# FFN tiles whose last step stands behind the next tile's partial sums, a convolution whose steps are spread later, and a pinned start with sixteen idle matmuls

## The chip, the core and the metric

The kernel runs on one core of a Trainium2 chip. The metric is the device time of one launch in microseconds. A core has five instruction streams that run side by side, each in its own order: TensorE (PE, matmuls), VectorE (DVE), ScalarE (ACT), GpSimd (POOL) and SyncE (SP, here a queue of DMA transfers; ACT issues some too). An instruction waits until what it reads has been written and what it overwrites has been read, and everything behind it in the same stream waits with it.

## What is computed

Two transformer-like blocks over 1024 positions and 1024 channels, in float32. Only the first is touched by more than a name; its part that matters, from the reference:

```python
h = rmsnorm(x, g_mix[i])
z = jnp.einsum("bsd,dn->bsn", h, w_in[i])
...
a = a_val * jax.nn.sigmoid(a_gt)
a = causal_dwconv(a, conv_a_w[i]) + conv_a_b[i]      # 31 taps, 512 channels
a = jax.nn.silu(layernorm(a, ln_a_g[i], ln_a_b[i]))
y_a = jnp.einsum("bsc,cd->bsd", a, w_a_out[i])
s = sc_b * causal_dwconv(sc_c * sc_v, conv_b_w[i])   # 3 taps
y_b = jnp.einsum("bsc,cd->bsd", s, w_b_out[i])
x = x + jnp.einsum("bsd,de->bse", g_a * y_a + g_b * y_b, w_o[i])
h = rmsnorm(x, g_ffn[i])
u = jnp.einsum("bsd,df->bsf", h, w_up[i])
f_gate = causal_dwconv(u[..., :D_FF], conv_f_w[i]) + conv_f_b[i]    # 3 taps, D_FF = 2816
f = jax.nn.gelu(f_gate, approximate=True) * u[..., D_FF:]
x = x + jnp.einsum("bsf,fd->bsd", f, w_down[i])
```

## The kernel before

Channels lie on the 128 partitions, positions along the free axis, in two halves of 512. Every product is made exact enough by splitting both operands into a high and a low part (wh, wl for weights; hh, hl and the like for data): three fp32r matmuls of 128x512 for each pair of blocks (lines 134 to 136, `mm3`). A weight comes by DMA into a buffer `wr` (5 of them), ACT copies it to wh, and DVE or POOL subtracts to give wl.

*The start.* SP loads the small vectors (`vec`, 325 columns, line 103), then for each of 8 channel blocks a weight (line 261) and half of x (line 262); the second half of x follows (line 268). ACT writes w0h (L264) and hh (L154), DVE writes w0l (L265) and hl (L155), and PE runs the first products `agt`.

*The convolutions.* The 31 taps of the long convolution are 30 steps of DVE on a whole row of 1024 for each of 4 tiles (`acc`, line 321) after one first step on ACT (L330). They are put into a queue; `bg(n)` takes n of them, so the numbers in the calls say where they stand between the other work. That other work is: `scc`, `scv`, `scb` products for 4 tiles, evicted by DVE into `cc` (L533, L539) and `sv` (L548), with a short convolution (first step on ACT, L328; two steps on DVE, L321; a multiplication on POOL, L543) between; then `split` of the four `sv` into sph (ACT, L151) and spl (DVE, L152), which are the operands of the products `yb`, eight times with a `gate` product ahead of each. The LayerNorm of the long convolution stands behind in the same queue of steps and is needed by the products `ya` after the gates.

*The FFN.* 22 tiles of 128 channels of both halves of `w_up`. A tile's four blocks are multiplied with a scheme of seven products instead of eight (a0, b0, b1, t4, t1, t2, t3; `quad`), each of 12 matmuls. The sums of weights that the scheme needs are four POOL additions (L635 to L638, for the tile after), and the weights are split in four groups, named here by their buffers qa (a0, t2), qb (t3, t1), qc (b0, b1) and qe (t4): ACT L151 and DVE L152. Products share PSUM banks, with additions on DVE between (L686: the u2, u4, c21, c22 and the second half of ug). PE's order in a tile is t2, t3, t1, b0, b1, t4, then a0 of the next. What becomes of a tile is `ff_tile`: ug is scaled (DVE L724 and L686, POOL L727), convolved with 3 taps (ACT L330, two DVE steps L321), put through Gelu (ACT L741), scaled (POOL L742), multiplied with c21 and c22 (DVE L744, two halves) and stored by a DMA of ACT's queue (`f_spill`, L745). The framework's scheduler turns the written order into the order on each engine, mostly by when an instruction was written.

Of the kernel before, what the change touches and what calls it, by code (L numbers as in the profile page):

```python
# [11 lines left out]
F32 = mybir.dt.float32  # L12
# [8 lines left out]
P = 128  # L21
# [3 lines left out]
KD = D // P  # L25
# [30 lines left out]
def block_kernel(ctx: ExitStack, tc: tile.TileContext, a: dict, out: bass.AP, dbg=None):  # L56
# [45 lines left out]
    vec = const.tile([P, NV], F32, name="vec")  # L102
    nc.sync.dma_start(out=vec, in_=a["vecs"])

# [7 lines left out]
    G.memset(ones, 1.0)  # L112
    junk = const.tile([P, CTX], F32, name="junk")


# [141 lines left out]

    w0 = [[slot("w0" + q, F32R, (P, 2, H2)) for _ in range(KD // 2)] for q in "hl"]
    for k in range(KD):
        raw = wtile("wr", (P, H2), F32, NWR)  # L260
        nc.sync.dma_start(out=raw, in_=a["w_in0"][k])
        nc.sync.dma_start(out=xs[0][k], in_=a["xT"][k * P : (k + 1) * P, hs(0)])
        hi, lo = (w[k // 2][:, k % 2, :] for w in w0)
        S.activation(out=hi, in_=raw, func=AF.Copy)  # L264
        V.tensor_tensor(out=lo, in0=raw, in1=f32(hi), op=ALU.subtract)  # L265
        split(h1[k][0][:, hs(0)], h1[k][1][:, hs(0)], xs[0][k], v("g_mix", k))
    for k in range(KD):
        nc.sync.dma_start(out=xs[1][k], in_=a["xT"][k * P : (k + 1) * P, hs(1)])
    first = [[bank("agt") for _ in range(4)], [None] * 4]

# [257 lines left out]
    for i in range(4):  # L528
        w = load_w(a["w_in"][12 + i], KD, lo_eng=G)
        cc = slot("cc")  # L530
        for h in range(2):
            ps = gemm(w, h1, h, "scc")
            V.tensor_tensor(out=cc[:, hs(h)], in0=ps, in1=rb[:, hs(h)], op=ALU.mult)  # L533
            G.tensor_tensor(out=cc[:, hs(h)], in0=cc[:, hs(h)], in1=rb[:, hs(h)], op=ALU.mult)
        bg(6)
        w = load_w(a["w_in"][16 + i], KD, lo_eng=G)
        for h in range(2):
            ps = gemm(w, h1, h, "scv")
            V.tensor_tensor(out=cc[:, hs(h)], in0=ps, in1=cc[:, hs(h)], op=ALU.mult)  # L539
        sv[i] = slot("sv")  # L540
        for f in conv_steps(cc, sv[i], "conv_b_w", 3, i):
            f()
        G.tensor_tensor(out=sv[i], in0=sv[i], in1=rb, op=ALU.mult)  # L543
        bg(4)
        w = load_w(a["w_in"][8 + i], KD, lo_eng=G)
        for h in range(2):
            ps = gemm(w, h1, h, "scb")
            V.tensor_tensor(out=sv[i][:, hs(h)], in0=ps, in1=sv[i][:, hs(h)], op=ALU.mult)  # L548
        bg(6)

    def gate(j):
        w = load_w(a["w_in"][20 + j], KD, lo_eng=G)
        g = slot("gate")
        for h in range(2):
            ps = gemm(w, h1, h, "gate")
            V.tensor_tensor(out=g[:, hs(h)], in0=ps, in1=rb[:, hs(h)], op=ALU.mult)
            S.activation(out=g[:, hs(h)], in_=g[:, hs(h)], func=AF.Sigmoid, bias=v("b_gate", j))
        return g

# [5 lines left out]
    for j in range(KD):  # L565
        g = gate(8 + j)
        bg(5)
        w = load_w(a["w_b_out"][j], 4, lo_eng=G, small_w=True)
# [6 lines left out]
    for j in range(KD):  # L575
        gA.append(gate(j))
        bg(6)
    while bgq:
# [132 lines left out]

    def quad(w, ug, x):

        y, z, u = (bank("q") for _ in range(3))
        m1, u2, u4, c21, c22 = (half_t("qm") for _ in range(5))
# [5 lines left out]
        padd(u4, y, m1)  # L721
        padd(c22, z, u4)
        product(x, w, "b0", True)
        V.tensor_tensor(out=ug[:, hs(0)], in0=x, in1=rb2[:, hs(0)], op=ALU.mult)  # L724
        product(u, w, "b1")
        padd(ug[:, hs(1)], u, u4)
        G.tensor_tensor(out=ug[:, hs(1)], in0=ug[:, hs(1)], in1=rb2[:, hs(1)], op=ALU.mult)  # L727
        product(z, w, "t4", True)
        padd(c21, z, u2)
        return c21, c22  # L730

    def begin(j):
        w, x = load_quad(a["w_upq"][j]), bank("q")
        product(x, w, "a0")
        return w, x

    def ff_tile(j, ug, cs):
        fa = slot("fa")
        for f in conv_steps(ug, fa, "conv_f_w", 3, j, v("conv_f_b", j)):
            f()  # L740
        S.activation(out=fa, in_=fa, func=AF.Gelu_apprx_tanh)  # L741
        G.tensor_tensor(out=fa, in0=fa, in1=rb2, op=ALU.mult)  # L742
        for h in range(2):
            V.tensor_tensor(out=fa[:, hs(h)], in0=cs[h], in1=fa[:, hs(h)], op=ALU.mult)  # L744
# [3 lines left out]
    cs = quad_first(wq0, ug)  # L748
    w, x = begin(1)
    st.spread(rb2, (1,))  # L750
    V.tensor_tensor(out=ug, in0=ug, in1=rb2, op=ALU.mult)
    ff_tile(0, ug, cs)
    for j in range(1, N_FF):
        ug = slot("ug")
        cs = quad(w, ug, x)
        if j + 1 < N_FF:
            w, x = begin(j + 1)
        ff_tile(j, ug, cs)
    def load_f(k):
# [232 lines left out]
    po_spill = dram.tile([512, T], F32, name="po_spill")  # L992
    cinv = const.tile([P, 4, 16], F32, name="cinv")
    nc.sync.dma_start(out=cinv, in_=a["cinv"])
    for i in range(4):
# [73 lines left out]
    def rope_table(row):  # L1069

        tab = slot("rtab", F32, (P, 2, 512))
        nc.sync.dma_start(out=tab, in_=a["rope"][row])
        g = const.tile([P, 64], F32, name=f"rg{row}")
        nc.sync.dma_start(out=g, in_=a["rope_g"][row])
        rg = const.tile([P, 64], F32, name=f"rgr{row}")
# [435 lines left out]
```

## Time and profile before

| | |
|---|---|
| median of 3 runs | 2020.9 us (2017.68 to 2021.72) |
| the profiled execution, its own time | 2018.58 us |
| its span (first to last instruction) | 2016.8 us |
| PE busy | 1936.9 us, 96% of the span, 8926 matmuls |
| DVE busy | 1374.4 us, 68% |
| ACT busy | 701.5 us, 35% |
| POOL busy | 608.4 us, 30% |
| DMA | 186.11 MB, mean 92 GB/s |
| granted TensorE clock, mean | 0.993 of full |

PE is busy nearly throughout, so what counts is where it isn't. Busy time is a rough word for PE: matmuls are pipelined, and a matmul that is reported with 0.39 us starts 0.23 us after the one before it. Lost time shows as idle time ahead of a matmul, as a larger distance between starts, or as a lower granted clock.

### The profile page before, as it was taken

The page shows a single profiled execution, that of the slowest core. Times are in us where ns is not written, and L with a number is a line of the kernel's source. Part 1 is how long each engine was busy: PE and PEld are TensorE (multiplying, and loading weights), DVE is VectorE, ACT ScalarE, POOL GpSimd, SP SyncE. Part 2 cuts the span into 40 slices and gives each one's busy share as a digit, 9 for nine tenths or more (in the row PEclk, how much of TensorE's full clock was granted, in tenths as well). Part 3 has the DMA queues.
Part 4 walks back from the last instruction along what each step waited for, and adds up shares of the span by engine and source line. Part 5 has one row for each costly group of instructions (what it writes and reads, how often), then busy time and mean ns, then how long its engine had stood idle before and what let it go on. Part 6 is the DMA issues. An engine that isn't in the chain of part 4 may idle for free.

```text
span 2016.8 us, 23964 instructions
## 1 busy us (share of the span) xinstructions
PE 1936.9 (96%) x8926; PEld 1575.9 (78%) x8926; DVE 1374.4 (68%) x2219; ACT 701.5 (35%) x1172; POOL 608.4 (30%) x417
## 2 busy tenths in 40 slices
PE   8999979999999999999998999999999999999999
PEld 6788758788877777777776787878777888888887
DVE  5799897345668765665655449996889476878751
ACT  5211121233344332332324312355442256556510
POOL 1334521131002545455451010223354322323200
PEclk9999989999999999999999999999999999999999
DMA  6011212212442222222225436544331221001151
GB/s 214 24 50 37 63 58 74 73 42 94 148 149 89 79 78 68 87 65 79 78 71 180 172 118 200 180 142 143 109 126 62 71 76 45 14 14 43 34 191 47
DMA packets 76468, 186.11 MB, mean 92 GB/s; under 512 B 8640, under 2 KB 15424, under 8 KB 76352
## 3 DMA queue, kind: packets, MB, share of 16 engines
q1 hardware_dynamic: 67856, 162.04, 24.9%
q10 hardware_dynamic: 8496, 22.55, 2.8%
q8 instruction: 70, 1.15, 0.2%
q14 instruction: 46, 0.38, 0.1%
HBM read 149.42 MB, written 35.13 MB: 92 GB/s over the span
## 4 chain that ended last, share of the span: by engine, by line
PE 48%; DVE 24%; issue 14%; POOL 6%; ACT 5%; DMA 3%; ACTq 0%; SPq 0%; POOLq 0%; DVEq 0%
DVE acc L321 6%; PE gate L135 3%; PE gate L134 3%; PE gate L136 3%; PE wd L135 2%; PE wd L136 2%; POOL ug L727 2%; PE wd L134 2%; POOL wr L635 2%; PE pv L1322 2%; DVE mj L432 2%; PE wout L134 1%; DVE wr L929 1%; PE wout L136 1%; PE wo L134 1%
## 5 line engine op out<-in xcount | busy, mean ns | idle before, releaser
L129 ACT ACTIVATE wh<-wr 128x1024 fp32r<-128x1024 f32 (+2 forms) x116 | 115.6, 997 | 342.5 <-PE wd L135 84.1
L130 POOL TENSOR_TENSOR wl<-wr,wh 128x1024 fp32r<-128x1024 f32 x44 | 115.8, 2634 | 269.3 <-ACT wh L129 249.1
L321 DVE SCALAR_TENSOR_TENSOR acc<-av,vec,acc 128x1023 f32<-128x1023 f32 (+14 forms) x120 | 192.0, 1600 | 4.3 <-ACT acc L330 1.7
L134 PE MATMUL q<-t,wh 128*128 128x512 f32 x352 | 140.5, 399 | 22.8 <-DVE qm L686 22.4
L151 ACT ACTIVATE wh<-wr 128x1024 fp32r<-128x1024 f32 (+1 forms) x92 | 84.5, 938 | 167.3 <-PE q L136 145.8
L135 PE MATMUL wd<-fl,wh 128*128 128x512 f32 x352 | 138.4, 395 | 2.6 <-DVE fl L763 2.5
L152 DVE TENSOR_TENSOR wl<-wr,wh 128x1024 fp32r<-128x1024 f32 (+1 forms) x92 | 113.9, 1239 | 37.7 <-ACT wh L151 37.6
L135 PE MATMUL q<-t,wh 128*128 128x512 f32 x352 | 138.9, 395 | 0.2 <-DVE t L152 0.2
L136 PE MATMUL q<-t,wl 128*128 128x512 f32 x352 | 138.7, 394 | 0.0
L136 PE MATMUL wd<-fh,wl 128*128 128x512 f32 x352 | 138.5, 395 | 0.0
L134 PE MATMUL wd<-fh,wh 128*128 128x512 f32 x352 | 132.5, 397 | 3.3 <-ACT fh L762 3.2
L221 POOL TENSOR_TENSOR ss<-ss,sq 128x512 f32<-128x512 f32 x42 | 62.3, 1499 | 201.5 <-ACT sq L220 201.5
L635 POOL TENSOR_TENSOR wr<-wr 128x512 f32<-128x512 f32 x22 | 45.2, 2053 | 208.6 <-DVE wl L152 101.8
L134 PEld LDWEIGHTS q<-t,wh 128*128 128x128 f32 x352 | 66.1, 188 | 46.6 <-issue 29.3
L134 PE MATMUL gate<-hh,wh 128*128 128x512 f32 x256 | 101.5, 396 | 0.0
L135 PE MATMUL gate<-hl,wh 128*128 128x512 f32 x256 | 101.1, 395 | 0.0
L136 PE MATMUL gate<-hh,wl 128*128 128x512 f32 x256 | 100.7, 393 | 0.0
L130 DVE TENSOR_TENSOR wl<-wr,wh 128x1024 fp32r<-128x1024 f32 (+2 forms) x72 | 83.8, 1164 | 16.2 <-ACT wh L129 15.1
L321 DVE SCALAR_TENSOR_TENSOR fa<-ug,vec,fa 128x1023 f32<-128x1023 f32 (+1 forms) x44 | 58.2, 1324 | 49.5 <-ACT fa L330 49.5
L744 DVE TENSOR_TENSOR fa<-qm,fa 128x512 f32<-128x512 f32 x44 | 28.4, 687 | 93.2 <-POOL fa L742 93.2
L1297 POOL TENSOR_SCALAR wr<-wr,rsum 128x1280 f32<-128x1280 f32 x32 | 43.0, 1345 | 145.6 <-DVE rsum L1296 128.2
L135 PEld LDWEIGHTS wd<-fl,wh 128*128 128x128 f32 x352 | 66.1, 188 | 20.2 <-DVE fl L763 4.4
(464 smaller groups left out, 5517.9 us busy)
## 6 DMA issues: line engine op xcount, KB each, us to landing
wr<-in_w_upq SPq DMA_DIRECT2D x88, 256.0 KB, 3.3
wr<-in_w_in SPq DMA_DIRECT2D x32, 512.0 KB, 3.4
wm<-in_w_modT SPq DMA_DIRECT2D x48, 256.0 KB, 3.0
f_spill<-fa ACTq DMA_DIRECT2D x22, 512.0 KB, 2.6
fl<-f_spill SPq DMA_DIRECT2D x22, 512.0 KB, 5.5
x<-in_xT SPq DMA_DIRECT2D x32, 256.0 KB, 4.5
wr<-in_w_o SPq DMA_DIRECT2D x16, 512.0 KB, 3.5
x_spill<-x ACTq DMA_DIRECT2D x32, 256.0 KB, 2.0
```

The lines of the kernel that those rows point to most:

```text
L129: S.activation(out=hi, in_=raw, func=AF.Copy)
L130: lo_eng.tensor_tensor(out=lo, in0=raw, in1=f32(hi), op=ALU.subtract)
L134: PE.matmul(ps, lh, rh, start=start, stop=False, **kw)
L135: PE.matmul(ps, lh, rl, start=False, stop=False, **kw)
L136: PE.matmul(ps, ll, rh, start=False, stop=stop, **kw)
L151: S.activation(out=hi, in_=src, func=AF.Copy)
L152: V.tensor_tensor(out=lo, in0=src, in1=f32(hi), op=ALU.subtract)
L221: eng.tensor_tensor(out=self.sums[:, hs(h)], in0=self.sums[:, hs(h)], in1=q, op=ALU.add)
L321: V.scalar_tensor_tensor(out=acc[:, s:T], in0=src[:, 0 : T - s], scalar=w, in1=acc[:, s:T], op0=ALU.mult, op1=ALU.add)
L432: V.scalar_tensor_tensor(out=half_t("mj"), in0=mm[n], scalar=1.0, in1=cb[ci][h], op0=ALU.mult, op1=ALU.mult, accum_out=modh[:, h, ci, j : ...
L635: G.tensor_tensor(out=s1, in0=a21, in1=a22, op=ALU.add)
L1297: G.tensor_scalar(out=pm, in0=pm, scalar1=rs, scalar2=1.0, op0=ALU.mult, op1=ALU.mult)
```

## The change

*The start.* Only the 8 columns of `vec` that the start needs (g_mix) are loaded first; the other 317 come after the second pair of loads. The loads are written under a manual order for SP, so that weights and x alternate to the end, and the small tables `cinv` and `rope_g`, which were loaded far later, are loaded there. Sixteen matmuls of 128x128 on a tile of ones, into a bank that nobody reads, stand first on PE.

*The convolutions.* `bg(6), bg(4), bg(6)` around the short convolutions become 5, 3, 5; `bg(5)` after a gate of `yb` becomes 4; in the later gates `bg(6)` behind each becomes three steps inside each half.

*The FFN.* `ff_tile` is cut into `ff_conv` (convolution, Gelu, POOL's scaling) and `ff_end` (multiplication with c21, c22 and the store). `ff_end` of a tile is written inside the next tile's `quad`, behind its u4 and c22. `begin(j + 1)`, the load, the sums and the product a0 of the next tile, is written ahead of t4.

```diff
@@
-    nc.sync.dma_start(out=vec, in_=a["vecs"])
+    nc.sync.dma_start(out=vec[:, 0:KD], in_=a["vecs"][:, 0:KD])
...
+    idle = bank("idle")
+    for _ in range(16):
+        PE.matmul(idle[:, 0:P], ones, ones, start=True, stop=True)
...
+    order = tc.manual_schedule(engines={mybir.EngineType.SP})
+    order.__enter__()
     for k in range(KD):
...
+        if k == 1:
+            nc.sync.dma_start(out=vec[:, KD:NV], in_=a["vecs"][:, KD:NV])
...
+    cinv = const.tile([P, 4, 16], F32, name="cinv")
+    nc.sync.dma_start(out=cinv, in_=a["cinv"])
+    rope_g = [const.tile([P, 64], F32, name=f"rg{row}") for row in range(2)]
+    for row in range(2):
+        nc.sync.dma_start(out=rope_g[row], in_=a["rope_g"][row])
+    order.__exit__(None, None, None)
...
-        bg(6)
+        bg(5)
...
-        bg(4)
+        bg(3)
...
-        bg(6)
-
-    def gate(j):
+        bg(5)
+
+    def gate(j, steps=0):
...
+            bg(steps)
...
-        bg(5)
+        bg(4)
...
-        gA.append(gate(j))
-        bg(6)
+        gA.append(gate(j, 3))
...
-    def quad(w, ug, x):
+    def quad(j, w, x, prev):
...
         padd(u4, y, m1)
         padd(c22, z, u4)
+        ff_end(*prev)
         product(x, w, "b0", True)
...
+        nxt = begin(j + 1) if j + 1 < N_FF else None
         product(z, w, "t4", True)
         padd(c21, z, u2)
-        return c21, c22
...
-    def ff_tile(j, ug, cs):
+        return ug, (c21, c22), nxt
+
+    def ff_conv(j, ug):
         fa = slot("fa")
...
         G.tensor_tensor(out=fa, in0=fa, in1=rb2, op=ALU.mult)
+        return fa
+
+    def ff_end(j, fa, cs):
         for h in range(2):
             V.tensor_tensor(out=fa[:, hs(h)], in0=cs[h], in1=fa[:, hs(h)], op=ALU.mult)
         nc.scalar.dma_start(out=f_spill[j * P : (j + 1) * P, :], in_=fa)
...
     for j in range(1, N_FF):
-        ug = slot("ug")
-        cs = quad(w, ug, x)
-        if j + 1 < N_FF:
-            w, x = begin(j + 1)
-        ff_tile(j, ug, cs)
+        ug, cs, nxt = quad(j, *nxt, prev)
+        prev = j, ff_conv(j, ug), cs
+    ff_end(*prev)
```

What the engines are given moves as follows. (In the rows, a name's number tells one buffer from another; the width after it is the shape.)

DVE in the convolution stage, just ahead of the last short convolution (`sv`), before; a step `acc` of width 1024 - s is step s of the third tile:

```order
L539 TENSOR_TENSOR cc_1391<-scv_1458,cc_1391 128x512
L321 SCALAR_TENSOR_TENSOR acc_714<-av_661,vec,acc_714 128x1006
L321 SCALAR_TENSOR_TENSOR acc_714<-av_661,vec,acc_714 128x1005
L321 SCALAR_TENSOR_TENSOR acc_714<-av_661,vec,acc_714 128x1004
L539 TENSOR_TENSOR cc_1391<-scv_1484,cc_1391 128x512
L321 SCALAR_TENSOR_TENSOR acc_714<-av_661,vec,acc_714 128x1003
L321 SCALAR_TENSOR_TENSOR sv_1510<-cc_1391,vec,sv_1510 128x1023
```

The same place of DVE in the changed kernel:

```order
L553 TENSOR_TENSOR cc_1409<-scv_1475,cc_1409 128x512
L335 SCALAR_TENSOR_TENSOR acc_741<-av_688,vec,acc_741 128x1015
L335 SCALAR_TENSOR_TENSOR acc_741<-av_688,vec,acc_741 128x1014
L335 SCALAR_TENSOR_TENSOR acc_741<-av_688,vec,acc_741 128x1013
L553 TENSOR_TENSOR cc_1409<-scv_1501,cc_1409 128x512
L335 SCALAR_TENSOR_TENSOR acc_741<-av_688,vec,acc_741 128x1012
L335 SCALAR_TENSOR_TENSOR sv_1527<-cc_1409,vec,sv_1527 128x1023
```

The last `sv` follows step 12 of the third tile instead of step 21. In ACT's order, the first step of that tile (which the others wait for) now stands behind the last `wsh`, a small weight of `yb` that waits for its DMA; before, it stood two such weights earlier.

POOL in one turn of the FFN loop, before; `ug` and `fa` are of the tile just computed, the four `wr` rows are the sums for the next:

```order
L727 TENSOR_TENSOR ug_5478<-ug_5478,rb_427_3382 128x512
L635 TENSOR_TENSOR wr_5707<-wr_5709 128x512
L637 TENSOR_TENSOR wr_5707<-wr_5706,wr_5709 128x512
L636 TENSOR_TENSOR wr_5706<-wr_5707,wr_5706 128x512
L638 TENSOR_TENSOR wr_5708<-wr_5708,wr_5706 128x512
L742 TENSOR_TENSOR fa_5608<-fa_5608,rb_427_3382 128x1024
```

POOL in the same turn of the changed kernel:

```order
L748 TENSOR_TENSOR ug_5502<-ug_5502,rb_428_3409 128x512
L759 TENSOR_TENSOR fa_5635<-fa_5635,rb_428_3409 128x1024
L649 TENSOR_TENSOR wr_5721<-wr_5723 128x512
L651 TENSOR_TENSOR wr_5721<-wr_5720,wr_5723 128x512
L650 TENSOR_TENSOR wr_5720<-wr_5721,wr_5720 128x512
L652 TENSOR_TENSOR wr_5722<-wr_5722,wr_5720 128x512
```

POOL's scaling of `fa` has moved ahead of the four sums.

DVE in the same turn, before, from the second half of `ug` on; the `qm` rows are in turn c21, u2, u4 and c22, the `wl` rows the splits of qb, qc and qe:

```order
L686 TENSOR_TENSOR ug_5478<-q_5481,qm_5484 128x512
L152 TENSOR_TENSOR wl_5584<-wr_5568,wh_5583 128x1024
L321 SCALAR_TENSOR_TENSOR fa_5608<-ug_5478,vec,fa_5608 128x1023
L686 TENSOR_TENSOR qm_5485<-q_5480,qm_5483 128x512
L152 TENSOR_TENSOR wl_5588<-wr_5569,wh_5587 128x1024
L321 SCALAR_TENSOR_TENSOR fa_5608<-ug_5478,vec,fa_5608 128x1022
L686 TENSOR_TENSOR qm_5622<-q_5618,qm_5621 128x512
L152 TENSOR_TENSOR wl_5592<-wr_5570,wh_5591 128x512
L744 TENSOR_TENSOR fa_5608<-qm_5485,fa_5608 128x512
L744 TENSOR_TENSOR fa_5608<-qm_5486,fa_5608 128x512
L686 TENSOR_TENSOR qm_5623<-q_5618,qm_5621 128x512
L686 TENSOR_TENSOR qm_5625<-q_5619,qm_5623 128x512
```

DVE in the same turn of the changed kernel:

```order
L700 TENSOR_TENSOR ug_5502<-q_5505,qm_5508 128x512
L156 TENSOR_TENSOR wl_5598<-wr_5582,wh_5597 128x1024
L335 SCALAR_TENSOR_TENSOR fa_5635<-ug_5502,vec,fa_5635 128x1023
L335 SCALAR_TENSOR_TENSOR fa_5635<-ug_5502,vec,fa_5635 128x1022
L700 TENSOR_TENSOR qm_5509<-q_5504,qm_5507 128x512
L156 TENSOR_TENSOR wl_5602<-wr_5583,wh_5601 128x1024
L700 TENSOR_TENSOR qm_5646<-q_5642,qm_5645 128x512
L156 TENSOR_TENSOR wl_5606<-wr_5584,wh_5605 128x512
L764 TENSOR_TENSOR fa_5635<-qm_5509,fa_5635 128x512
L764 TENSOR_TENSOR fa_5635<-qm_5510,fa_5635 128x512
L700 TENSOR_TENSOR qm_5647<-q_5642,qm_5645 128x512
L700 TENSOR_TENSOR qm_5649<-q_5643,qm_5647 128x512
```

The two convolution steps now stand together, ahead of c21 and of the split of qc; the two multiplications stay where they were, ahead of u4 and c22. On ACT, Gelu moves ahead of the split of qc (before: split of qc, copy of a0, Gelu, split of qe). On PE, a0 of the next tile comes before t4; the number of matmuls in a turn stays 84.

## Rows read from the trace of the kernel before

**Rows 1.** Windows: PE, PEld, DVE, ACT, POOL busy us (instructions), clock, DMA share, GB/s.

```profile
100.00:250.00 150.00, 150.00 (x650) 121.90 (x649) 131.93 (x98) 20.34 (x21) 66.13 (x27) 1.00 0.17 51
250.00:300.00 50.00, 36.34 (x136) 27.02 (x135) 46.69 (x39) 12.97 (x15) 13.35 (x6) 0.83 0.17 58
660.00:1080.00 420.00, 397.55 (x1696) 316.54 (x1695) 252.77 (x286) 128.01 (x143) 217.72 (x117) 1.00 0.25 79
```

**Rows 2.** Timeline, the start, PE: start, us, operation, [idle before <- releaser].

```profile
8.01 1.22 PE L134 MATMUL agt<-hh,w0h 128*128 128x512 f32 x2 [8.01 <-ACT hh L154]
...
13.30 0.52 PE L134 MATMUL agt<-hh,w0h 128*128 128x512 f32 x1
13.65 0.39 PE L135 MATMUL agt<-hl,w0h 128*128 128x512 f32 x1
...
34.01 0.50 PE L135 MATMUL agt<-hl,w0h 128*128 128x512 f32 x1 [0.78 <-DVE hl L155]
```

**Rows 3.** Timeline, convolution stage: ACT and DVE up to the last short convolution.

```profile
223.47 0.64 ACT L129 ACTIVATE wsh<-wr 128x512 fp32r<-128x512 f32 x1 [8.74 <-DMA wr<-in_w_b_out]
...
226.88 3.90 DVE L321 SCALAR_TENSOR_TENSOR acc<-av,vec,acc 128x1017 f32<-128x1017 f32 x3
...
231.30 8.13 DVE L321 SCALAR_TENSOR_TENSOR acc<-av,vec,acc 128x1014 f32<-128x1014 f32 x4
...
252.35 0.69 DVE L539 TENSOR_TENSOR cc<-scv,cc 128x512 f32<-128x512 f32 x1
...
253.07 1.15 ACT L328 ACTIVATE sv<-cc,vec 128x1024 f32<-128x1024 f32 x1 [23.70 <-DVE cc L539]
```

**Rows 4.** Timeline, PE: first product yb and the gate behind it.

```profile
255.22 0.50 PE L134 MATMUL yb<-sph,wsh 128*128 128x512 f32 x1 [4.55 <-ACT sph L151]
...
268.88 0.79 PE L134 MATMUL yb<-sph,wsh 128*128 128x512 f32 x1 [3.00 <-ACT sph L151]
...
274.77 0.40 PE L134 MATMUL gate<-hh,wh 128*128 128x512 f32 x1
```

**Rows 5.** Timeline, one FFN turn, all engines, from one product t4 to the next.

```profile
809.28 0.47 PE L134 MATMUL q<-t,wh 128*128 128x512 f32 x1 [1.28 <-DVE qm L686]
...
811.15 0.68 DVE L686 TENSOR_TENSOR ug<-q,qm 128x512 f32<-128x512 f32 x1
...
811.74 1.21 DVE L152 TENSOR_TENSOR wl<-wr,wh 128x1024 fp32r<-128x1024 f32 x1
811.90 2.21 POOL L727 TENSOR_TENSOR ug<-ug,rb 128x512 f32<-128x512 f32 x1 [5.42 <-DVE ug L686]
...
814.14 1.24 ACT L330 ACTIVATE fa<-ug,vec 128x1024 f32<-128x1024 f32 x1 [3.82 <-POOL ug L727]
...
820.76 1.29 POOL L637 TENSOR_TENSOR wr<-wr,wr 128x512 f32<-128x512 f32 x1
...
821.34 1.26 DVE L152 TENSOR_TENSOR wl<-wr,wh 128x512 fp32r<-128x512 f32 x1 [1.11 <-ACT wh L151]
...
825.08 2.40 POOL L742 TENSOR_TENSOR fa<-fa,rb 128x1024 f32<-128x1024 f32 x1
...
827.52 1.29 DVE L744 TENSOR_TENSOR fa<-qm,fa 128x512 f32<-128x512 f32 x2 [4.92 <-POOL fa L742]
...
830.29 0.47 PE L134 MATMUL q<-t,wh 128*128 128x512 f32 x1 [1.26 <-DVE qm L686]
```

**Rows 6.** Groups by shape, 660 to 1080 us: count, busy us, mean ns, idle before.

```profile
L152 DVE TENSOR_TENSOR wl<-wr,wh 128x1024 fp32r<-128x1024 f32 x60 | 75.0, 1249 | 5.5 <-ACT wh L151 5.5
...
L151 ACT ACTIVATE wh<-wr 128x1024 fp32r<-128x1024 f32 x60 | 61.3, 1050 | 153.8 <-PE q L136 141.6 <-issue 8.0 <-PE q L135 4.1
...
L321 DVE SCALAR_TENSOR_TENSOR fa<-ug,vec,fa 128x1023 f32<-128x1023 f32 x20 | 26.7, 1334 | 47.0 <-ACT fa L330 47.0
...
L741 ACT ACTIVATE fa<-fa 128x1024 f32<-128x1024 f32 x21 | 22.3, 1062 | 59.4 <-DVE fa L321 59.4
```

More of the change, by code (lines that the diff above doesn't have):

```diff
@@ L710, in quad_first, with begin @@
         return c21, c22
-    def quad(w, ug, x):
+    def begin(j):
+        w, x = load_quad(a["w_upq"][j]), bank("q")
+        product(x, w, "a0")
+        return w, x
+    def quad(j, w, x, prev):
+        ug = slot("ug")
         y, z, u = (bank("q") for _ in range(3))
@@ L727, in quad @@
         G.tensor_tensor(out=ug[:, hs(1)], in0=ug[:, hs(1)], in1=rb2[:, hs(1)], op=ALU.mult)
+        nxt = begin(j + 1) if j + 1 < N_FF else None
         product(z, w, "t4", True)
         padd(c21, z, u2)
-        return c21, c22
[L732 to L735, printed above, removed]
-    def ff_tile(j, ug, cs):
+        return ug, (c21, c22), nxt
+    def ff_conv(j, ug):
         fa = slot("fa")
@@ L748, in block_kernel @@
     cs = quad_first(wq0, ug)
-    w, x = begin(1)
+    nxt = begin(1)
     st.spread(rb2, (1,))
     V.tensor_tensor(out=ug, in0=ug, in1=rb2, op=ALU.mult)
-    ff_tile(0, ug, cs)
+    prev = 0, ff_conv(0, ug), cs
     for j in range(1, N_FF):
-        ug = slot("ug")
-        cs = quad(w, ug, x)
-        if j + 1 < N_FF:
-            w, x = begin(j + 1)
-        ff_tile(j, ug, cs)
+        ug, cs, nxt = quad(j, *nxt, prev)
+        prev = j, ff_conv(j, ug), cs
+    ff_end(*prev)
     def load_f(k):
@@ L992, in block_kernel @@
     po_spill = dram.tile([512, T], F32, name="po_spill")
-    cinv = const.tile([P, 4, 16], F32, name="cinv")
-    nc.sync.dma_start(out=cinv, in_=a["cinv"])
     for i in range(4):
@@ L1072, in rope_table @@
         nc.sync.dma_start(out=tab, in_=a["rope"][row])
-        g = const.tile([P, 64], F32, name=f"rg{row}")
-        nc.sync.dma_start(out=g, in_=a["rope_g"][row])
+        g = rope_g[row]
         rg = const.tile([P, 64], F32, name=f"rgr{row}")
```

## The prediction

> **What bounds the kernel now.** I read the windows first, for where TensorE is not at its rate. From 100 to 250 us it runs 650 matmuls in 150 us, one every 0.231 us, and is never idle [rows 1]; that is its rate, and any stretch with fewer matmuls has lost the difference. The reader should find three such stretches that the change touches. From 250 to 300 us there are 136 matmuls where 217 would fit, so 81 x 0.231 = 18.7 us are lost, and the granted clock is 0.83 [rows 1]. In the FFN loop, 660 to 1080 us, 20 turns take 420 us; the timeline gives 830.29 - 809.28 = 21.0 us for one turn [rows 5], while its 84 matmuls need 84 x 0.231 = 19.4 us. At the start the first matmul comes at 8.01 us, and 5.29 us pass until the one at 13.30, the thirteenth, 0.44 us each; then 0.35 and soon 0.23 [rows 2].
>
> Then I read the timeline of each stretch for what comes last. In the convolution stage TensorE waits for sph and spl of the short convolutions [rows 4], ACT is held for 23.70 us by the last cc of DVE, and that eviction starts only at 252.35, between long steps of acc [rows 3]. TensorE had that product long before; DVE is late because it is full (131.93 of 150 us busy [rows 1]). In the FFN turn TensorE waits 1.26 us at t4 for the c22 of DVE. DVE was held 4.92 us by POOL's fa, which started at 825.08 because four sums stood ahead of it [rows 5], although Gelu was done before 821. So the loop is bound by a ring DVE, POOL, ACT, DVE, POOL, DVE, PE, and not by TensorE.
>
> One more thing is to be seen in the rows: a DVE operation on two SBUF operands and a POOL operation do not run at once. DVE's wl takes its 1.21 us from 811.74, and POOL's ug, from 811.90, is given 2.21 where the same shape takes 1.29 at 820.76; wl of 128x512 at 821.34 takes 1.26, as long as one of twice its width, and ends after that POOL operation [rows 5].
>
> **The change part by part.** *Start.* If TensorE is at full rate when the first product comes, 12 matmuls save 12 x (0.44 - 0.231) = 2.5 us [rows 2]. No row has a float32 matmul of this shape beside an idle start; the sixteen last between 16 x 0.06 = 1 us (the 0.231 scaled to 128 columns) and 16 x 0.44 = 7 us, and only if they last until near the first product does the rate hold. I take the 2.5, with 0 as the other end. The stall at 34.01, 0.78 us on hl [rows 2], should shrink, as x of the first half is no longer queued behind weights that wait for buffers: 0.5 us, between 0 and 1.5. The small tables that are now loaded early are 128x64 each, at a point where SP has sent all of x; I cost them at nothing. Sum 3 us, between 0 and 5.
>
> *Convolutions.* The steps of acc before the last sv fall from 21 to 12. They cannot start at once: their first step on ACT now follows the last wsh, which landed at 223.47 and took 0.64 [rows 3]; with that first step (1.24, as the one of the FFN at 814.14 [rows 5]) DVE starts at 225.4. Eleven steps and three evictions of 0.6 come before the last cc. A step takes 3.90 / 3 = 1.30 us beside an idle POOL and 8.13 / 4 = 2.03 beside a working one [rows 3]. So the cc would start between 225.4 + 14.3 + 1.8 = 241.5 and 225.4 + 22.3 + 1.8 = 249.5, against 252.35. I take the middle, 245.4: as many POOL operations (the scaling of cc, the splits) lie there as before, over fewer steps. Everything behind it (sv on ACT at 253.07, sph, yb at 255.22 and 268.88, the gate at 274.77 [rows 3, 4]) hangs on it and moves by the same 7 us, between 3 and 11. The nine steps put off run later beside gates, where nothing of TensorE needs DVE but evictions. The LayerNorm behind them slides later but still lies ahead of the products ya by several gates of 48 matmuls, about 11 us each; without that cover the nine steps would come back, 9 x 1.3 = 12 us.
>
> *FFN loop.* Time is counted from the start of the add that ends ug (811.15 in the turn shown). POOL starts ug 0.75 later, as before [rows 5], and takes 1.3, if no wl goes first: 2.05. ACT's first step 1.24 [rows 5]: 3.3. Two steps on DVE, now together, 1.3 each: 5.9. Gelu 1.06: 7.0. POOL's fa, nothing ahead of it now, 2.40: 9.4 [rows 5, 6]. The old wait for four sums is gone, and with it the wait of 4.92. What is late next? ACT splits qc after Gelu, 1.05 [rows 6], so DVE's wl of qc is asked for at 8.05, while POOL is in fa. It waits until 9.4, takes 1.2, and u2 behind it takes 0.68: 11.3. Product t1 needs u2, since it goes on in the same bank. From there TensorE has t1, b0, b1, 36 matmuls of 0.231, 8.3 us, and the next ug add follows in 0.3: 19.9 to 20.0.
>
> A second ring is about as long. After the wl of qc (10.6) POOL's sums and DVE's wl of qe and two multiplications alternate: 1.3, 0.6, 1.3, 0.7, 1.3, 0.7 = 5.9, so 16.5. ACT's store stands behind these and ahead of the split of qa (1.05: 17.6); DVE has u4 and c22 (1.4: 17.9), then wl of qa, 1.2, with the last sum of POOL against it up to 0.5 more, 19.1 to 19.6; then the first half of ug, 0.6: 19.7 to 20.2. I take 20.1 us for a turn, so 0.9 less, over 20 turns 18 us. The stall moves from t4 to t1, some 0.5 us. a0 ahead of t4 costs nothing by itself: the weights of qa are ready at about 19.5 and a0 starts at 19.9, but that cover is thin, and each 0.1 us that it lacks costs 2 us.
>
> Here the Trainium skill has a rule that speaks against the new order: "SBUF — State Buffer", section "SBUF: two separate sides", says that VectorE with two SBUF inputs and GpSimd take a shared pair of ports as an exclusive lock, for the whole instruction, and the loser blocks fully. By it, fa ahead of wl of qc holds TensorE's next operand back, as in the sum above; if the two only shared, wl would end near 9.3 and t1 would not wait, which is the first rival below. The trace agrees with the lock (2.21 against 1.29).
>
> **Sum.** 3 + 7 + 18 = 28 us off the profiled execution's 2018.6: 1990.6. That execution lies 2.3 us below the median and within the runs (2017.68 to 2021.72); I forecast 1991.
>
> **The rivals.** *TensorE alone bounds the loop.* If POOL's fa or the sums take less than I gave them, a turn takes 19.5, and 30 us are saved there: 2018.6 - 40 = 1979. For it speaks that the rings are only 0.5 us too long; against it, that POOL's 2.40 for fa is the figure of a row with hardly a DVE operation beside it. Chance 0.14.
>
> *The race after ug.* DVE's wl of qb and POOL's ug both become ready around 0.8 us: wl needs ACT's split, which follows the last matmul of b1 by 1.05 us (0.9 on this clock), POOL is ready at 0.75. Before, wl went first in the row at 811.74 [rows 5]. If it goes first in each turn, the ring is 1.2 us longer, 21.3: the loop is 6 us slower, start and convolutions save 10, and the time is 2015; with half of the turns, 2003. Chance 0.15.
>
> *Slower: wl of qc loses to the sums too.* POOL now goes from fa straight into the sums. If it takes the ports again before the waiting wl, each sum ahead costs 1.3 us at t1 in all 20 turns, 26 us. With two sums a turn takes 22.7: 2018.6 - 10 + 34 = 2043. It is slower from a turn of 21.7 on, or 1.2 sums on the mean. Against it: at 821.34 wl was let in after one POOL operation, although more sums were queued [rows 5]. Chance 0.06.
>
> *The start and the convolutions don't do what they say.* The idle matmuls end too early or the rate falls again, and DVE takes back in later evictions what the short convolutions gain: 18 us remain, 2000.6. Chance 0.07.
>
> **How the numbers follow.** My forecast, turns of 19.8 to 20.5 us and the other two parts within their bounds, has 0.58 and runs from about 1981 to 2000. The range 1979 to 2012 reaches to most of the race and to the edge of TensorE's bound, and leaves out the slower case, the race lost in every turn, and half of the first rival, some 0.17. A measurement of this kernel can tell about 0.2% from no change, 4 us. Faster by more than that: the forecast, the first rival, the fourth, and most of the race, 0.87. Within it: the race lost in all turns, or one sum ahead of wl, 0.07. Slower: 0.06.
>
> **What would show it.** Starts of the first ug add of each turn 20.1 us apart; no idle time at t4, some 0.5 us at t1 with u2 as its releaser; POOL's fa right after Gelu and ahead of the sums; POOL's ug near 1.3 us instead of 2.21 (if it stays at 2.2, the race is lost). The last cc near 245 and the gate behind the first yb near 268. The first products 0.23 us apart. Turns of 21 us or more, or a wait of a0 for its weights, would make the forecast wrong.

## The result, and the profile after

The changed kernel takes 1998.08 us (median of 4 runs, 1996.59 to 2000.13); the kernel before took 2019.29 us beside it. The ratio is 0.9895, with a 95% interval of 0.9878 to 0.9912: about 21 us less. The profiled execution's span fell from 2016.8 to 1996.8 us, so the 20.0 us can be looked for in the two traces. The forecast was 1991: the direction and the range held the result, and 7 us of the gain did not come.

The three stretches of [rows 1], now (the FFN loop begins and ends some 10 us earlier, so its window is moved; columns as there):

```profile
100.00:250.00 150.00, 147.28 (x636) 118.97 (x634) 123.40 (x93) 25.28 (x26) 69.50 (x29) 1.00 0.14 48
...
250.00:300.00 50.00, 44.60 (x176) 35.21 (x177) 35.81 (x33) 11.06 (x14) 13.66 (x7) 0.87 0.24 80
...
650.00:1070.00 420.00, 412.23 (x1752) 327.37 (x1751) 353.02 (x299) 137.54 (x151) 199.43 (x118) 1.00 0.26 86
```

From 250 to 300 us there are 176 matmuls instead of 136, in the loop 1752 instead of 1696 in the same 420 us. DVE's busy time in the loop rose by 100 us although it does the same work in a turn (some 5% more turns lie in the window): its operations now stand beside POOL's for longer, and a blocked operation counts as busy (its splits of 128x1024 take 1.98 us on the mean instead of 1.25, the multiplications with c21 and c22 1.67 instead of 0.69).

The start (timeline of TensorE; to be read beside [rows 2]):

```profile
1.13 6.66 PE L117 MATMUL idle<-ones 128*128 128x128 f32 x32 [1.13 <-POOL ones L112]
7.55 1.18 PE L138 MATMUL agt<-hh,w0h 128*128 128x512 f32 x4
8.57 0.40 PE L139 MATMUL agt<-hl,w0h 128*128 128x512 f32 x1
8.81 0.39 PE L140 MATMUL agt<-hh,w0l 128*128 128x512 f32 x1
```

The idle matmuls (two records for each) fill the time up to the first product, 0.42 us each, and the products are 0.23 us apart from the start.

The convolution stage (DVE, then TensorE; beside [rows 3, 4]):

```profile
239.59 0.69 DVE L553 TENSOR_TENSOR cc<-scv,cc 128x512 f32<-128x512 f32 x1
...
251.92 0.80 PE L139 MATMUL yb<-spl,wsh 128*128 128x512 f32 x1 [4.64 <-DVE spl L156]
...
256.16 0.80 PE L138 MATMUL yb<-sph,wsh 128*128 128x512 f32 x1 [3.02 <-ACT sph L155]
...
263.35 0.40 PE L138 MATMUL gate<-hh,wh 128*128 128x512 f32 x1
```

The last cc comes 12.8 us sooner than at 252.35, the gate behind the first yb 11.4 us sooner than at 274.77; 5.2 us of both were already there at the products av, from the start. The wait of 4.55 us ahead of the first yb is gone; the one of 3.0 us for the last sph is as long as before, and the one for the last spl is 4.64 us instead of 3.96.

One FFN turn (DVE, POOL and TensorE by time; beside [rows 5]):

```profile
801.70 0.69 DVE L700 TENSOR_TENSOR ug<-q,qm 128x512 f32<-128x512 f32 x1 [0.50 <-PE q L140]
...
802.48 1.29 POOL L748 TENSOR_TENSOR ug<-ug,rb 128x512 f32<-128x512 f32 x1 [3.56 <-DVE ug L700]
...
802.63 2.22 DVE L156 TENSOR_TENSOR wl<-wr,wh 128x1024 fp32r<-128x1024 f32 x1 [0.23 <-ACT wh L155]
...
808.92 2.40 POOL L759 TENSOR_TENSOR fa<-fa,rb 128x1024 f32<-128x1024 f32 x1 [5.15 <-ACT fa L758]
...
809.82 2.58 DVE L156 TENSOR_TENSOR wl<-wr,wh 128x1024 fp32r<-128x1024 f32 x1 [1.53 <-ACT wh L155]
...
812.33 0.68 DVE L700 TENSOR_TENSOR qm<-q,qm 128x512 f32<-128x512 f32 x1
...
813.06 0.50 PE L138 MATMUL q<-t,wh 128*128 128x512 f32 x1 [0.24 <-DVE qm L700]
...
821.71 0.69 DVE L700 TENSOR_TENSOR ug<-q,qm 128x512 f32<-128x512 f32 x1 [0.50 <-PE q L140]
```

From one ug add to the next 20.01 us pass, where it was 21.0. POOL's ug goes first and takes 1.29 us, DVE's wl of qb behind it 2.22: the race after ug is won (POOL's ug takes 1.29 or 1.30 us in 19 of the loop's 21 turns). POOL's fa follows Gelu at once. DVE's wl of qc, asked for at 809.8, takes 2.58 us because fa runs until 811.3; u2 (812.33) and t1 (813.06) follow. That is the first ring of the prediction, step by step. The stall has left t4, and 0.24 us of it is left at t1, TensorE's only wait in this turn; a0 does not wait for its weights.

Where the rest went is read from the start of each stage in both traces. A second execution of each kernel is beside them, profiled later:

| start of | before | before, again | after | after, again | after less before, this stage |
|---|---|---|---|---|---|
| av | 59.97 | 61.62 | 54.77 | 54.83 | -5.2 |
| gate behind the first yb | 274.77 | 276.70 | 263.35 | 263.00 | -6.2 |
| ya | 485.70 | 487.62 | 477.20 | 476.82 | +2.9 |
| first product q | 623.36 | 625.27 | 616.75 | 616.37 | +1.9 |
| first half of ug, tile 1 | 661.47 | 666.67 | 659.30 | 658.85 | +4.4 |
| first product wd | 1086.83 | 1089.96 | 1067.78 | 1067.35 | -16.9 |
| first product pg | 1340.74 | 1345.78 | 1323.69 | 1322.19 | +2.0 |
| end of the span | 2016.8 | 2018.4 | 1996.8 | 1995.5 | -2.9 |

The last column adds up to -20.0. The three parts of the change gave 28.3 us, all that was forecast; three stages that the sum had at nothing cost 9.2 us. The last two rows are no effect that can be told: two executions of the same kernel before differ there by as much (from pg to the end 676.1 and 672.6 us). The split between tile 1 and the loop isn't firm either. In the second execution of before, tile 1 starts 3.3 us later after the first q than in the first, and the first two turns of the loop give 2.2 of them back (41.9 us instead of 44.1). Between the two second executions the loop's stage gains 14.8 us instead of 16.9, tile 1 loses 1.1 instead of 4.4, and the three stages together cost 5.9 instead of 9.2.

All three losses lie at or just behind a `spread`, where TensorE itself needs four products of DVE (dg, an identity times the new scale). Before, TensorE had no wait at the LayerNorm's. The second half of it, now:

```profile
428.79 2.96 DVE L201 TENSOR_SCALAR dg<-ident,rc 128x128 f32<-128x128 f32 x4
429.07 2.40 POOL L134 TENSOR_TENSOR wl<-wr,wh 128x1024 fp32r<-128x1024 f32 x1 [2.44 <-ACT wh L133]
431.80 1.12 PE L207 MATMUL sp<-dg,ones 128*128 128x512 f32 x2 [2.33 <-DVE dg L201]
```

The first half of the FFN's norm, first after, then before:

```profile
593.46 3.90 DVE L201 TENSOR_SCALAR dg<-ident,rc 128x128 f32<-128x128 f32 x4
597.42 1.94 PE L207 MATMUL sp<-dg,ones 128*128 128x512 f32 x2 [1.99 <-DVE dg L201]
...
600.01 0.63 PE L140 MATMUL wo<-mix,wl 128*128 128x512 f32 x1
600.44 0.63 PE L138 MATMUL wo<-mix,wh 128*128 128x512 f32 x1
```

```profile
601.68 3.91 DVE L197 TENSOR_SCALAR dg<-ident,rc 128x128 f32<-128x128 f32 x4
605.65 1.13 PE L203 MATMUL sp<-dg,ones 128*128 128x512 f32 x2 [2.02 <-DVE dg L197]
...
607.08 0.40 PE L136 MATMUL wo<-mix,wl 128*128 128x512 f32 x1
607.31 0.39 PE L134 MATMUL wo<-mix,wh 128*128 128x512 f32 x1
```

Here products and wait are as long before as after, so DVE takes nothing back. What differs is the granted TensorE clock behind the wait: 0.57 of full from 597 to 601 us, 1.00 from 605 to 609 in the trace before. So the 1.9 us are the clock's. The drop behind this wait shows in five of the six executions that have the steps spread and DVE's products here, and in none of the four without the spreading; in the sixth, the split of qc ahead of Gelu (below), the program up to here is the changed kernel's and the wait is 2.0 us too, but 1.00 is granted from 597 to 601. It goes with the spreading mostly, not always, and why is not shown.

And the second half of the FFN's norm, first after, then before:

```profile
641.35 1.26 POOL L649 TENSOR_TENSOR wr<-wr 128x512 f32<-128x512 f32 x1 [15.76 <-DVE rc L180]
641.36 3.96 DVE L201 TENSOR_SCALAR dg<-ident,rc 128x128 f32<-128x128 f32 x4
642.57 1.26 POOL L651 TENSOR_TENSOR wr<-wr,wr 128x512 f32<-128x512 f32 x1
...
645.47 2.04 PE L207 MATMUL sp<-dg,ones 128*128 128x512 f32 x2 [4.19 <-DVE dg L201]
```

```profile
647.93 0.87 DVE L197 TENSOR_SCALAR dg<-ident,rc 128x128 f32<-128x128 f32 x4
648.67 1.28 POOL L635 TENSOR_TENSOR wr<-wr 128x512 f32<-128x512 f32 x1 [16.48 <-DMA wr<-in_w_upq]
648.95 1.10 PE L203 MATMUL sp<-dg,ones 128*128 128x512 f32 x2 [1.09 <-DVE dg L197]
```

Four small products take 0.87 us when POOL is idle. If POOL's first sum starts with them, three of the four each wait for one sum (1.3 us instead of 0.28) and the four take 3.96. Of the 4.4 us here 3.1 are the longer wait; behind it the granted clock is 0.66 from 645 to 650 us, where the trace before shows 1.00 from 648 to 653. In the trace before, the sums came 0.74 us later than the products did. In its second execution they came 0.31 us later, the products took 2.90 us and TensorE waited 3.12.

### The profile page after: what moved, and what is told of

Same layout as the page of the kernel before. It is cut to its first block, busy times and chain, and to the rows that moved or that the text cites. A ratio compares the mean times of both kernels' runs of the same rounds, so it can differ in the third digit from the quotient of the medians.

```text
span 1996.8 us, 24031 instructions
## 1 busy us (share of the span) xinstructions
PE 1944.2 (97%) x8958; PEld 1581.6 (79%) x8958; DVE 1457.3 (73%) x2219; ACT 705.3 (35%) x1172; POOL 591.1 (30%) x417
## 4 chain that ended last, share of the span: by engine, by line
PE 75%; DVE 12%; issue 6%; ACT 4%; POOL 2%; DMA 1%; ACTq 0%; DVEq 0%; SPq 0%; POOLq 0%
PE q L138 4%; PE wd L139 4%; PE wd L140 4%; PE wd L138 3%; PE q L139 3%; PE q L140 3%; PE gate L139 3%; PE gate L138 3%; PE gate L140 3%; DVE fa L335 2%; PE pv L1338 2%; PE wo L138 2%; PE wout L140 1%; PE wout L139 1%; PE wo L139 1%
## 5 line engine op out<-in xcount | busy, mean ns | idle before, releaser
L134 POOL TENSOR_TENSOR wl<-wr,wh 128x1024 fp32r<-128x1024 f32 x44 | 119.8, 2724 | 276.0 <-ACT wh L133 264.4
L156 DVE TENSOR_TENSOR wl<-wr,wh 128x1024 fp32r<-128x1024 f32 (+1 forms) x92 | 159.8, 1737 | 49.7 <-ACT wh L155 49.6
L335 DVE SCALAR_TENSOR_TENSOR acc<-av,vec,acc 128x1023 f32<-128x1023 f32 (+14 forms) x120 | 186.5, 1554 | 10.2 <-ACT acc L344 7.5
L759 POOL TENSOR_TENSOR fa<-fa,rb 128x1024 f32<-128x1024 f32 x22 | 53.6, 2436 | 120.3 <-ACT fa L758 120.3
L138 PEld LDWEIGHTS wd<-fh,wh 128*128 128x128 f32 x352 | 66.7, 190 | 21.0 <-ACT fh L781 5.1
L140 PEld LDWEIGHTS wd<-fh,wl 128*128 128x128 f32 x352 | 66.5, 189 | 15.8
```

The costliest lines, as they stand in the source:

```text
L134: lo_eng.tensor_tensor(out=lo, in0=raw, in1=f32(hi), op=ALU.subtract)
L138: PE.matmul(ps, lh, rh, start=start, stop=False, **kw)
L140: PE.matmul(ps, ll, rh, start=False, stop=stop, **kw)
L156: V.tensor_tensor(out=lo, in0=src, in1=f32(hi), op=ALU.subtract)
L335: V.scalar_tensor_tensor(out=acc[:, s:T], in0=src[:, 0 : T - s], scalar=w, in1=acc[:, s:T], op0=ALU.mult, op1=ALU.add)
```

## The experiments

**Each part alone.** The edits are three parts of the diff shown above, each on the kernel before: the start, with the idle matmuls, the pinned loads and the small tables; the `bg` numbers and `gate`; `quad`, `begin` and the two halves of `ff_tile`.

> The kernel before with the start alone (idle matmuls, loads pinned, small tables early). Theory (each part gains on its own, and the whole loses some 9 us again where four 128x128 products of DVE for a spread meet POOL operations while TensorE waits): the products av begin about 5 us earlier, at 55 instead of 60.0, and the whole is 3 to 5 us faster, less what such a meeting happens to take back. Rival (the gain of the start is swallowed by the convolution stage, since DVE sets its end): av 5 us earlier, but the gate behind the first yb at 274 to 275 as before, and no gain in the whole.

Measured: 2017.95 us against 2019.54, ratio 0.9991 (0.9981 to 1.0001), not clear of no change. In its trace av begins at 54.70 and the gate behind the first yb at 269.43, so the 5.3 us reach that gate, and against the rival DVE does not swallow them; they are there at the first q (618.01). Then 4.4 us go at the spread ahead of tile 1, with a wait of 4.2 us; the first two turns of the loop give 2.2 of them back.

> The kernel before with the steps of the long convolution spread later, alone. Theory: the gate behind the first yb 6 to 7 us earlier (274.8 to about 268.5); the spread of the LayerNorm, now later, again waits for its four products on DVE if a POOL split runs beside them, 2 to 3 us; the whole 3 to 6 us faster. Rival (the 6 us at the gate come from the start's five, and the spreading alone gives little): gate at 272 or later, the whole within 1 us of before.

Measured: 2017.98, ratio 0.9987 (0.9978 to 0.9996). The gate behind the first yb comes at 267.46, 7.3 us earlier; by ya 4.6 us of it are gone, at the LayerNorm's spread (2.6 us of waiting, and a granted clock of 0.50 behind it, from 437 to 440 us); 4.4 us go ahead of tile 1. The theory holds for the stage; for the whole it was at best just met (the interval allows 0.8 to 4.4 us), since it left out the second place.

> The kernel before with the new order of the FFN loop alone. Theory: turns of 20.0 us instead of 20.9, the loop 18 to 20 us shorter, the whole 17 to 20 us faster. Rival (the loop's gain in the whole kernel is partly the first turn's, and 2 to 4 us of the 18 are lost again at the loop's end): the whole 13 to 15 us faster, with the loss at the first products wd.

Measured: 2004.98, ratio 0.9927 (0.9903 to 0.9952), 14.6 us. The turns are 20.0 us, as the theory has it, but the whole is the rival's. From the first q to the first wd it gains 15.2 us: the 17 turns in between bring 0.98 us each, and the last turn and the way from it to wd give 2.7 back (18.40 + 8.6 us from one first half of ug to the next and to wd, against 17.34 + 6.96). In this trace the products ahead of tile 1 do not meet the sums. The ratios of the three parts add up to 0.95% against 1.05% for the whole.

**The four products elsewhere.** First all of them on ACT:

```diff
-            V.tensor_scalar(out=d[:, i * P : (i + 1) * P], in0=ident, scalar1=r[:, i : i + 1], scalar2=None, op0=ALU.mult)
+            S.activation(out=d[:, i * P : (i + 1) * P], in_=ident, func=AF.Copy, scale=r[:, i : i + 1])
```

> The changed kernel with the four 128x128 products ahead of each spread on ACT instead of DVE. Theory (they are held up by POOL operations on DVE, TensorE waits at the spread and then runs some matmuls at half rate): the waits of 2.3 us at the LayerNorm's spread, 2.0 us at the first spread of the FFN's norm and 4.2 us at the second shrink to under 1 us each, and the whole is 6 to 10 us faster than the changed kernel, near 1989. Rival (the chain of small operations ahead, or ACT's own queue, is as late): the waits stay within 1 us of what they are and the whole within 2 us of the changed kernel.

Measured: 1995.99, ratio 0.9878 (0.9859 to 0.9898), 2 to 3 us less than the changed kernel, and not clear of it (the intervals overlap): for the whole the rival's. The stages say where:

```profile
423.57 2.45 ACT L201 ACTIVATE dg<-ident,rc 128x128 f32<-128x128 f32 x8 [1.89 <-DVE rc L180]
...
427.37 1.88 PE L207 MATMUL sp<-dg,ones 128*128 128x512 f32 x4
...
636.49 2.05 PE L207 MATMUL sp<-dg,ones 128*128 128x512 f32 x2 [1.90 <-ACT qm L716]
```

At the LayerNorm the wait is gone, and ya comes 3.7 us earlier than in the changed kernel; at the first half of the FFN's norm it is gone too, and the first q is 7.6 us earlier. At the second half TensorE waits 1.9 us for ACT, by the profile for its copy `qm`, and not for the products. Then the first turns of the loop lose 3 us (its second and third steps take 20.29 and 21.63), and from pg to the end 5.5 us are lost (two executions of before differ there by 3.4).

Then only at four places, by an argument that names the engine (the last pair is the norm behind wd):

```diff
-        ln["st"].rstd(512)
+        ln["st"].rstd(512, eng=S)
...
-                st.rstd(D, (0,))
+                st.rstd(D, (0,), S)
...
-                st.rstd(D, (1,))
+                st.rstd(D, (1,), G)
...
-                st.rstd(D, (0,))
+                st.rstd(D, (0,), S)
```

> The changed kernel with the four products ahead of a spread on another engine only where the profile shows a wait: ACT for the LayerNorm, for the first half of the FFN's norm and for the first half of the norm behind the products wd; POOL for the second half of the FFN's norm; all others on DVE as before. Theory (the places gain what they gained with all of them on ACT, 3 to 4 us each, and the second block no longer loses 5 us): ya about 3 us earlier than in the changed kernel, the first product q 7 us, the whole 8 to 12 us faster than the changed kernel, near 1988. Rival (what the first block gains, the FFN loop or the second block loses again whatever engine has them): the whole within 3 us of the changed kernel.

Measured: 1997.16, ratio 0.9882 (0.9868 to 0.9897): the rival's. The first q is again 7.6 us earlier. POOL's four products take 2.34 us behind one of its own sums, TensorE waits 3.61 us there, and the first turns are as slow as in the run before. Behind the loop (where the norm of wd had been moved to ACT too) pg to utm takes 231.0 us against 224.7. So the place matters, not only the engine.

**What sets the turn.** One pair on ACT is exchanged; DVE's and POOL's orders stay as they are (`split` returns its operation on ACT, and the last tile's Gelu is left as it was; both are cut here).

```diff
-            split(hi, lo, q[:, 0:n, :])
+            hi_op = split(hi, lo, q[:, 0:n, :])
+            if q is qc:
+                ahead.append(hi_op)
...
-        S.activation(out=fa, in_=fa, func=AF.Gelu_apprx_tanh)
...
+            with tc.issue_after(ahead[-1].ins):
+                S.activation(out=fa, in_=fa, func=AF.Gelu_apprx_tanh)
```

> The changed kernel with one pair on ACT exchanged in each FFN turn: the split of qc (wh) ahead of Gelu instead of behind it; DVE's and POOL's orders stay. Theory (the turn of 20.0 us is set by DVE's wl of qc, which waits for the end of POOL's fa and holds u2 and t1): wl of qc now comes before POOL's fa and takes 1.2 us instead of 2.6, t1 no longer waits, a turn is 19.4 to 19.6 us, and the whole is 7 to 10 us faster than the changed kernel, near 1989. Rival (the second ring, over the sums, the split of qa and the first half of ug, is as long): a turn stays at 19.9 to 20.1 and the whole within 2 us of the changed kernel.

Measured: 1989.25, ratio 0.9843 (0.9828 to 0.9857), half a per cent less than the changed kernel. One turn (DVE, POOL):

```profile
797.18 0.69 DVE L705 TENSOR_TENSOR ug<-q,qm 128x512 f32<-128x512 f32 x1 [1.37 <-PE q L140]
...
803.68 1.22 DVE L156 TENSOR_TENSOR wl<-wr,wh 128x1024 fp32r<-128x1024 f32 x1
...
804.67 2.49 POOL L768 TENSOR_TENSOR fa<-fa,rb 128x1024 f32<-128x1024 f32 x1 [5.42 <-ACT fa L767]
...
805.62 0.69 DVE L705 TENSOR_TENSOR qm<-q,qm 128x512 f32<-128x512 f32 x1 [0.72 <-PE q L140]
...
816.69 0.69 DVE L705 TENSOR_TENSOR ug<-q,qm 128x512 f32<-128x512 f32 x1 [1.36 <-PE q L140]
```

The wl of qc takes 1.22 us, ahead of fa; u2 waits for TensorE instead of the other way round; a turn is 19.51 us, and TensorE has no wait at these products. So the wait for POOL's fa did set the turn, and the second ring is no longer than 19.5.

This edit together with the four places on other engines:

> The two edits together (split of qc ahead of Gelu; products ahead of the spreads moved where a wait was). Theory (they lie in different stages, so they add): 15 to 20 us faster than the changed kernel, near 1980. Rival (time saved in one place is taken back in another): less than 12 us.

Measured: 1987.54, ratio 0.9838 (0.9822 to 0.9854), 11 us less than the changed kernel: the rival's, and not clear of the run with the split of qc alone. The turns are 19.5 us and the products of POOL still hold TensorE for 3.8 us.

**The idle matmuls.**

```diff
-    for _ in range(16):
+    for _ in range(1):
```

> The changed kernel with one idle matmul in place of sixteen. Theory (the idle matmuls raise the rate before the first product): the first 12 or so products are 0.43 us apart instead of 0.23, and the products av begin 2 to 3 us later, at 57 to 58. Rival (the pinned loads alone give the start its 5 us): av within 0.7 us of 54.8.

Measured: one run, 2000.51; av begins at 57.38, 2.6 us later than in the changed kernel. The first products:

```profile
1.13 0.79 PE L117 MATMUL idle<-ones 128*128 128x128 f32 x2 [1.13 <-POOL ones L112]
8.27 1.22 PE L138 MATMUL agt<-hh,w0h 128*128 128x512 f32 x2 [6.34 <-ACT hh L158]
9.29 0.63 PE L139 MATMUL agt<-hl,w0h 128*128 128x512 f32 x1
9.71 0.63 PE L140 MATMUL agt<-hh,w0l 128*128 128x512 f32 x1
```

They are 0.43 us apart again: the thirteenth comes 4.78 us after the first, in the changed kernel 2.87, before 5.29. So the rate is worth 1.9 us here and 2.4 against the trace before. The other 0.7 us of the 2.6 are no rate: the first product itself begins at 8.27 instead of 7.55, and with the same loads and sixteen idle matmuls it begins between 7.47 and 8.51 in other runs, with when ACT's hh is ready. The rival, the loads alone, is out, but with one run of this kernel the share of each is known only to some tenths.

**The sums behind the products.** On top of the exchange on ACT:

```diff
-    nxt = begin(1)
+    held = small("held", 1)
+    hold = G.tensor_copy(out=held, in_=st.r[1][:, 4 * P - 1 : 4 * P])
+    with tc.issue_after(hold.ins):
+        nxt = begin(1)
```

> The kernel with the split of qc ahead of Gelu, and one more edit: POOL copies one element of the last of the four products ahead of the second spread of the FFN's norm, and the sums for the second FFN tile stand behind that copy, so that POOL can't run beside the four products. Theory (TensorE's wait of 4.2 us at that spread comes from the four products of DVE alternating with four sums of POOL): the four products take 0.9 us instead of 4.0, the wait falls to about 1 us, the matmuls behind it run at full rate, and the whole is 3 to 4.5 us faster than without the copy. Rival (later sums delay the second tile by as much): the wait falls and the loop's first turns grow by the same, no gain in the whole.

Measured: 1993.57, ratio 0.9858 (0.9839 to 0.9877), no faster than without the copy.

```profile
638.30 0.88 DVE L202 TENSOR_SCALAR dg<-ident,rc 128x128 f32<-128x128 f32 x4
...
639.24 0.19 POOL L779 COPY held<-dg 128x1 f32<-128x1 f32 x1 [40.58 <-DVE dg L202]
...
644.25 0.80 PE L138 MATMUL q<-a,wh 128*128 128x512 f32 x1 [5.63 <-ACT wh L155]
645.26 1.91 PE L208 MATMUL sp<-dg,ones 128*128 128x512 f32 x2
```

The four products take 0.88 us and end 6 us ahead of the spread: what held them, POOL's sums, is shown. But a0 of tile 1, which stands ahead of the spread, now waits 5.63 us for the weights made from the later sums. The wait has changed its place, as the rival said, though not to the turns it named.

And with that copy, the products of two of the spreads on ACT:

```diff
-        ln["st"].rstd(512)
+        ln["st"].rstd(512, eng=S)
...
-                st.rstd(D, (0,))
+                st.rstd(D, (0,), S)
```

> The same with the four products of the LayerNorm and of the first half of the FFN's norm on ACT; all spreads behind the FFN loop as in the changed kernel. Theory: 7 us faster than with the copy alone (3 at the LayerNorm, 4 at the first half of the norm), 10 to 11 us faster than the kernel with qc ahead of Gelu alone, near 1979. Rival (time saved ahead of the loop is taken back in its first turns): under 4 us faster.

Measured: 1981.28, ratio 0.9808 (0.9794 to 0.9823): 12 us less than the run with the copy alone, and 0.9% less than the changed kernel. It is the fastest of this study. ya comes at 474.18, the first q at 609.84, the first wd at 1052.71 (changed kernel: 477.20, 616.75, 1067.78), and with DVE kept for the norms behind the loop, pg to utm takes 224.8 us. The rival is out. Against the copy alone it is 12 us instead of the theory's 7: up to the first wd 6.9 us are gained, as the theory has it, and the rest comes behind, where the two programs are the same, and is not explained. Against the split of qc alone it is about 7 us (0.9808 against 0.9843) instead of 10 to 11; a0 of tile 1 still waits 5.61 us.

**Chance or program.**

> The changed kernel once more, for a second profile. If the meeting of products and sums at the FFN's second spread were chance of one execution (a transfer landing 0.7 us sooner or later), its wait may be 1 us here; if it belongs to the program's timing, it is 4.2 us again.

Measured: one run, 1997.36; the wait ahead of tile 1 is 4.17 us, as by the program's timing.

> The kernel before once more, for a second profile. By chance of one execution: the wait at the FFN's second spread, 1.1 us in the first profile, may be 4 us. By the program's timing: 1.1 us again.

Measured: one run, 2020.21; the wait there is 3.12 us instead of 1.09. So before, it was partly luck of the first profile that products and sums missed each other; in both profiles of the changed kernel, and in those of each of the first two parts alone, they met in full, and in that of the FFN loop alone they did not.

## Why the prediction was right, and where it was short

*The start* was mis-sized: 5.2 us instead of 3. The 2.5 of the rate came nearly (2.4 against the trace before, 1.9 by the run with one idle matmul). The term that was too small is the stall on hl: three stalls on hl of the second half went, not only part of the one shown, and with the slow matmuls behind them they had cost 2.2 us instead of the 0.5. The 0.5 us by which the first product came sooner lie within the spread of other runs. Which of the changes to the loads did it was not separated.

*The convolutions* were right in their mechanism and in size, the size partly by luck: 6.2 us for 7, the last cc 7.6 us sooner by this part for 7. In the run with this part alone the steps took longer than the middle that I took (eight of the eleven 2.04 us, three 1.30), but their chain began at 223.5 us instead of 225.4, as the last wsh came 1.7 us sooner. And from the last wait on sph to the gate it took 7.2 us instead of 5.9: the granted clock was 0.52 there, before 0.66. What failed is a sentence behind it, that the LayerNorm slides later but is needed only by ya, and so costs nothing. Its spread is a matmul in TensorE's own order and waits for DVE there. At its new place it stood beside a POOL split of 2.40 us, and 2.9 us were lost, 2.6 of them as waits. The cover that I named (gates ahead of ya) was the wrong one.

*The FFN loop* was right in its mechanism and nearly in size: turns of 20.0 for 20.1, 16.9 us for 18 (14.8 between the second executions). Every step of the first ring came within 0.3 us, and exchanging one pair on ACT took the ring away and gave the rival's turn, 19.5. In the turn shown the second ring, too, ended at 19.5, where 19.7 to 20.2 was forecast. The lock between DVE and POOL of "SBUF — State Buffer" (Trainium skill, section "SBUF: two separate sides") is borne out: 2.58 us beside fa, 1.22 ahead of it. The shortfall of 1.1 us lies at the end: the first two turns gave 3.0 (0.8 against the second execution of before), the 17 behind them 16.6, and the last one with the way to wd took 2.7 back, where I had counted 20 equal turns.

*What had no term* are places that the diff does not touch. At the first half of the FFN's norm 1.9 us went, where the wait is 2.0 us as before, but the matmuls behind it ran at half rate (0.43 us apart from 599.6 to 600.9, with the granted clock at its lower level): the clock's, which the sum had not considered. Ahead of tile 1 4.4 us went, of which 3.3 were luck of the first profile of before (its second shows 41.4 us from the first q to ug, where the first has 38.1); but with the 2.2 us that a late tile 1 gets back in the first two turns, that luck was worth 1.1 us. The fourth rival had the right kind of loss at the wrong place: the start and the convolutions gave what they should, and DVE held TensorE back at two spreads behind them.

*The rivals.* TensorE alone did not bound the loop; the race after ug was won in 19 of 21 turns; wl of qc waited for fa alone, the sums did not go ahead of it again.

What stays open: why, with the products on ACT, the loop's first turns are 3 us slower (in the first of these runs TensorE waits 0.86 and 1.77 us for additions of DVE there, and the granted clock is 0.50 from 688 to 691 us), why the second block lost 5 us with the norm behind wd there, and why the granted clock drops behind the wait of 2.0 us in some executions and not in others. Only the places are shown.

## What to carry to other kernels

When an edit shifts a stage, list every place behind it where TensorE waits for a short chain on another engine, and ask what will run beside that chain at its new time; gains of separate parts add up only as far as these places let them. Before a few us at one place are put down to a change, profile both kernels twice: here 3.3 of 4.4 us were chance, and 2.2 of them came back within two turns. An order on one engine can hold another through operations that exclude each other, although no semaphore joins them: here one pair exchanged on ACT was worth half as much as the whole change. To put work behind a barrier moves a wait to whoever needs that work.

## What the runs showed of the hardware

Four DVE products of 128x128 with one SBUF operand and a scalar from SBUF are held up by POOL as fully as those with two tensors: 0.87 us with POOL idle, 3.96 beside sums of 1.26 (three of the four products are held, 1.3 us each), 2.96 beside one split of 2.40 (one is held, 2.37 us). Where both engines have work queued, they take turns, one operation each: over the loop POOL's middle two sums take 1.75 us on the mean beside DVE's multiplications, and those 1.67 instead of 0.69. A float32 matmul of 128x128 beside an idle start shows as two records and takes 0.42 us, so sixteen of them last 6.7 us. Behind the same wait of TensorE of 2.0 us the granted clock fell to the lower of its two levels in the changed kernel (0.57 on the mean from 597 to 601 us) and stayed at the higher one with the split of qc ahead of Gelu (1.00).
